# DeltaNet's q, k, v and z products: hi weights against both source halves in one 512-column matmul, in groups of four

## The chip, the cores and the metric

The kernel runs on one core of a Trainium2 chip. The metric is the device time of one execution in microseconds (us); several runs are taken and their median is compared. Five engines work side by side, each through its own instructions in order: TensorE (PE; its weight loads are listed as PEld), VectorE (DVE), ScalarE (ACT), GpSimd (POOL) and SyncE (SP), which issues most of the transfers.

## The reference, cut to what matters

A two-layer decoder trunk on 256 tokens of 2048 features. Layer 0 mixes tokens with an mLSTM, layer 1 with a gated DeltaNet; each layer then attends to 256 memory tokens and applies a squared-ReLU MLP. The change touches the DeltaNet:

```python
def gdn_mixer(h, w_in, conv_w, a_log, dt_bias, norm_g, w_out):
    p = h @ w_in                                   # 256 x 2048 times 2048 x 12352
    qkv, z, bt, a = jnp.split(p, GDN_SPLITS, axis=-1)
    qkv = jax.nn.silu(causal_dwconv(qkv, conv_w))  # 4 taps along the tokens
    q, k, v = jnp.split(qkv, [2048, 4096], axis=-1)
    q, k = l2_norm(q) * GD_K ** -0.5, l2_norm(k)   # 16 key heads of 128
    ...
    A = jnp.einsum('...id,...jd->...ij', kb, kc) * jnp.exp(jnp.where(strict, diff, -jnp.inf))
    U = lax.linalg.triangular_solve(A, vb, left_side=True, lower=True, unit_diagonal=True)
    ...
    o = rms_norm(from_chunks(oc), norm_g) * jax.nn.silu(z)
    return o.reshape(B, S, GV_H * GD_V) @ w_out
```

q and k have 2048 features each, v and z 4096 each.

## The kernel before, in words

**Numbers in two parts.** Weights and activations are float32, and a product is made of three: each operand is split into hi (rounded to the format that TensorE takes at full rate) and lo (what is left), and hi·hi + hi·lo + lo·hi is summed in a bank of PSUM. A source tile `srcs[k]` holds 128 features: hi of the 256 tokens in columns 0 to 255, lo in 256 to 511 (`T` is 256).

**Weights.** `Weights` streams them in units of 1 MB. For the DeltaNet's q (but its first four blocks), k, v and z a unit is "tall": all 2048 rows, 128 columns. It arrives in two halves of 1024 rows (SP's queue, four raw buffers); ACT casts each to hi (line 88), VectorE subtracts to get lo (line 89). Two units of hi and two of lo fit, so that a unit is split while the one before it is used.

**Products.** `prod_tall` takes one tall unit per block of 128 features: for each of 16 row blocks it loads hi or lo weights and multiplies, three times 256 columns, all into the first half of one bank of 512 columns. There are five such accumulators. `prod_feat`, which serves the other feature-major products (q, k, o of the mLSTM, up of the MLP), already works on the bank in two halves, "wide": hi weights times the whole source tile (512 columns), lo weights times hi of the source into the second half; `join` then sums the halves, with a copy by ACT and an addition by VectorE. For a block that is not wide, `join` returns the bank's first half and issues nothing.

**What follows a block.** For q, k and v: `conv` reads the joined block, times 1/rms, into `pad` (VectorE, line 865), makes four taps of the convolution (one by ACT, 868, three by VectorE, 870) and a silu by ACT (871). For z: a product by VectorE (1189) and a silu by ACT (1190).

**Stages of the DeltaNet.** For four groups c of key heads, four blocks of q, then four of k. Between them `norms` (l2 norms, by squares on ACT, 960, and matmuls, 964) and `pairs`, which makes the blocks of A for four value heads: `decays` (matmuls gep, exponentials by ACT, 939), the products of k and q (matmuls g, 981 and 982), masks and products on VectorE (984, 986, 992). The last of these run between the first v blocks. Then come 32 blocks of v, with the triangular solver's 31 steps on VectorE (1051, 1054) between the blocks' convolutions, and transposes of v to DRAM (884). Last, twice: 16 blocks of z in four groups, each with the `core` of four heads (a chain np, xp, wp, cp, op, otp of small matmuls with ACT and VectorE between them), and the output product `g_out`.

**Order.** Each engine's order is fixed when the program is built, by a scheduler that lists instructions by when it reckons them ready; independent matmuls are laid between the dependent ones of `pairs` and `core`. A waiting instruction holds up what stands behind it on its engine.

Of the kernel before, what the change touches and what calls it, by code (L numbers as in the profile page):

```python
# [15 lines left out]
T = 256  # L16
# [18 lines left out]
class Weights:  # L35
    """Streams weight units [128, kb, n] from DRAM and splits each into hi + lo."""
# [8 lines left out]
    def add(self, key, w, k0, kn, n0, nn, tall=False):  # L45
        """Units of 512 rows and 512 columns or, tall, of all the rows and 128 columns (64 at most: hi and lo side
        by side)."""
        kk, un = (kn, P) if tall else (UK * P, UN)
        for n in range(n0, n0 + nn, un):
            w_n = min(un, n0 + nn - n)  # L50
            for k in range(k0, k0 + kn, kk):
                self.plan.append((key, w[k : min(k + kk, k0 + kn), n : n + w_n]))

    def begin(self, place=None):
        """Starts the next unit's loads; returns the two halves' splits, to be called in order.
        place(j) gives other tiles to hold the unit: hi and lo of its j-th 128 rows."""
# [54 lines left out]
def trunk(ctx: ExitStack, tc, x, mem, norm_g, mem_norm_g, w_mem_kv, w_xq, w_xo, w_up, w_down,  # L111
# [56 lines left out]
    # rows j, columns i: j <= i, j < i, j > i  # L168
    tri_le, tri_lt, tri_gt = mask("tri_le", ALU.is_ge, 1), mask("tri_lt", ALU.is_gt, 1), mask("tri_gt", ALU.is_gt, -1)

    def behind(ins, *others):
        """Issue order on an engine: ins after each of the others."""
# [4 lines left out]
    # per-feature vectors as columns [128 features, 128-blocks]  # L177
# [27 lines left out]
    def feed(tok, c, h, gains, then=None):  # L205
        """Features 512 c .. of a token-major tile (t, 512 features): feature-major, gained and split into h."""
# [13 lines left out]
    class Rms:  # L220
        """Sums of squares along the features of token-major tiles [128 tokens, 512] by ACT."""
# [18 lines left out]
    def split_into(dst, src, scale=None):  # L240
        """dst[:, 0:256] = round(scale * src), dst[:, 256:512] = what is left."""
# [14 lines left out]
    def token_sums(parts, name):  # L256
        """Sums over the partitions of the parts' sum, as columns [128 tokens, 2]."""
# [11 lines left out]
    def spread(dst, col0, col1):  # L269
        """dst[p, t] = the token's scalar on every partition."""  # L270
        for t, c in enumerate((col0, col1)):
            PE.matmul(dst[:, t * P : (t + 1) * P], c.to_broadcast([P, P]), ident, start=True, stop=True)

    class Bank:
        """A block of a product: complete in the first 256 columns, or two parts in the two halves (wide)."""
# [4 lines left out]
    def extra_unit(u0):  # L280
        """Prepares one more unit of weights in tiles of u that are free around the end of a sub-layer."""
# [10 lines left out]
    def prod_feat(key, srcs, n_fb, evac, wide=True, before=None, fresh=False):  # L292
        """Feature-major product: srcs[k] = [128, hi 256 | lo 256]; evac(fb, bank).
        fresh: the sources are only being made, each one's hi first."""
# [30 lines left out]
    def prod_tall(key, srcs, n_fb, evac, before=None):  # L325
        """Feature-major product by tall units, one block after the other."""
        for f in range(n_fb):
# [4 lines left out]
            for k in range(nk):  # L332
                PE.matmul(a[:, 0:T], hi[k], srcs[k][:, 0:T], start=(k == 0), stop=False)  # L333
                PE.matmul(a[:, 0:T], hi[k], srcs[k][:, T:], start=False, stop=False)  # L334
                m = PE.matmul(a[:, 0:T], lo[k], srcs[k][:, 0:T], start=False, stop=(k == nk - 1))  # L335
            evac(f, Bank(a, False))
        return m

    def prod_few(key, srcs):
        """Product with n <= 64 columns, token-major: [128 tokens, 2, n] in PSUM."""  # L340
# [5 lines left out]
        # [I I] sums the rows of hi and lo  # L346
# [7 lines left out]
    def prod_tok(key, srcs, n_ch, evac, after=None, post=None, stagger=False):  # L354
        """Token-major product: evac(chunk, token tile, acc [128 tokens, 512]).
        stagger: in the last chunk the first token tile takes two units before the second one does."""
# [30 lines left out]
    def join(b, name, n=P, dst=None):  # L387
        """A product's block, summed over the halves of its bank."""
# [28 lines left out]
    class Scales:  # L417
        """1/rms per token: as columns (tok) and spread over the partitions (row)."""
# [13 lines left out]
    class Post:  # L432
        """Collects a sub-layer's output, token-major, with the gain of its norm, and its sums of squares."""
# [17 lines left out]
        def take(self, ch, t, a, plus=False):  # L451
            """A finished piece of the product (plus: what is there already)."""
# [39 lines left out]
    def advance(post, nxt):  # L492
        """x += g * y / rms(y); returns the next sub-layer's gained, not yet normalised input, and x's Rms."""
# [113 lines left out]
    def mlstm(sc, h, rms, before):  # L607
# [23 lines left out]
        # log sigmoid(f) = -log1p(e), e = exp(-f) >= exp(-15)  # L631
# [8 lines left out]
        # decayed scores, as [s, t] blocks: 0 = (s0, t0), 1 = (s1, t1), 2 = (s0, t1)  # L640
# [42 lines left out]
        def head_out(hd):  # L683
# [11 lines left out]
            # 1 / max(|den|, 1) and the head's 1/rms  # L695
# [39 lines left out]
    def cross(sc, l, h, rms):  # L735
# [44 lines left out]
        prod_tall("xq", h, 1, lambda f, a: ev_q(XA_H - 1, a))  # L780
# [4 lines left out]
    def mlp_bias(rms):  # L785
        """What the norm of the product's input adds to the mean square of its output's: eps + eps / (its rms^2)."""
# [43 lines left out]
    def softplus(z, sc, n):  # L830
        """log(1 + exp(z)), with log1p's accuracy for small exponentials."""
# [15 lines left out]
    def gdn(g0, h, rms):  # L847
        # Over all 256 tokens: (I + A) w = v, o = B w, with
# [399 lines left out]
```

## Time and profile before

| | us |
|---|---|
| median of three runs (lowest, highest) | 2963.81 (2963.45, 2971.68) |
| the profiled execution, first to last instruction | 2962.9 |
| DeltaNet: q, k and pairs | 1230 to 1543 |
| DeltaNet: v and solver | 1543 to 1690 |
| DeltaNet: z, core and output product | 1690 to 2100 |

The profile's span leaves out what lies before the first and after the last instruction; the median stands 0.9 us above it. In a row of the timeline stand the start in us, the time in us, engine, line, operation, the tiles (out<-in) and the shape; in square brackets the idle time of the engine before it, and what ended that. A matmul's time reaches from its start to its last result, and the next one starts before that: the rate is read from the distance of the starts. A row of groups has count, busy time in us and mean time of one in ns, then idle time before them.

### The profile page before, as it was taken

What the parts mean: (1) busy time and instruction counts of PE and PEld (TensorE: products, weight loads), DVE (VectorE), ACT (ScalarE), POOL (GpSimd) and SP (SyncE); (2) the same over time, 40 slices, a digit from 0 to 9 for tenths busy, and PEclk for the clock granted to TensorE, in tenths of its full rate; (3) what the DMA queues carried; (4) which work ended last, traced back from release to release, by engine and by line L of the source; (5) the groups of instructions that cost most, each with busy time, mean ns of one, the idle gap of its engine ahead of it and who ended that gap; (6) DMA issues with size and microseconds to landing.
All of it is one profiled execution on the core that took longest, in us unless ns stands there. A gap on an engine that the chain in (4) does not pass through costs nothing.

```text
span 2962.9 us, 43790 instructions
## 1 busy us (share of the span) xinstructions
PE 2912.0 (98%) x17363; PEld 2545.9 (86%) x17363; DVE 1762.6 (59%) x2560; ACT 1449.7 (49%) x2245; POOL 137.1 (5%) x256
## 2 busy tenths in 40 slices
PE   8999999999999999999999999999999999999998
PEld 7888888988888888898889998899888888888887
DVE  5555657644545555677779745445567546455565
ACT  6454546544434344566655444444456444344343
POOL 0000000000000000013231111000000000000000
PEclk9999999999999999999999999999999999999999
DMA  7545565555555565556778955665445565565554
GB/s 237 175 154 164 190 197 163 171 195 186 189 194 185 195 189 189 180 143 188 198 210 223 268 168 176 209 183 165 163 150 184 186 196 183 193 191 189 189 191 168
DMA packets 423120, 553.27 MB, mean 187 GB/s; under 512 B 22769, under 2 KB 220914, under 8 KB 420610
## 3 DMA queue, kind: packets, MB, share of 16 engines
q1 hardware_dynamic: 412608, 507.12, 55.5%
q0 software_dynamic: 8736, 42.02, 4.3%
q8 instruction: 136, 2.23, 0.3%
q10 hardware_dynamic: 1570, 1.33, 0.1%
q14 instruction: 70, 0.57, 0.1%
HBM read 527.29 MB, written 23.10 MB: 186 GB/s over the span
## 4 chain that ended last, share of the span: by engine, by line
PE 92%; DMA 3%; DVE 3%; ACT 2%; issue 1%; DVEq 0%; ACTq 0%; SPq 0%
PE up L314 15%; PE up L315 8%; PE down L378 8%; PE down L380 8%; PE down L379 8%; DMA raw<-in_gdn_w_in 3%; PE gz L334 2%; PE gz L335 2%; PE gz L333 2%; PE g_out L378 2%; PE g_out L379 2%; PE g_out L380 2%; PE o L314 2%; PE gv L333 1%; PE gv L334 1%; PE gv L335 1%
## 5 line engine op out<-in xcount | busy, mean ns | idle before, releaser
L89 DVE TENSOR_TENSOR lo<-raw,hi 128x1024 fp32r<-128x1024 f32 x938 | 1122.8, 1224 | 888.0 <-ACT hi L88 886.6
L88 ACT CAST hi<-raw 128x1024 fp32r<-128x1024 f32 x938 | 950.4, 1046 | 980.8 <-PE down L380 310.8
L314 PE MATMUL up<-h,hi 128*128 128x512 f32 x1920 | 678.7, 399 | 0.0
L315 PE MATMUL up<-h,lo 128*128 128x256 f32 x1920 | 539.2, 281 | 0.0
L314 PEld LDWEIGHTS up<-h,hi 128*128 128x128 f32 x1920 | 360.8, 188 | 89.9
L379 PE MATMUL down<-lo,u 128*128 128x512 f32 x1024 | 398.4, 389 | 0.0
L378 PE MATMUL down<-hi,u 128*128 128x512 f32 x1024 | 398.4, 389 | 0.0
L380 PE MATMUL down<-hi,u 128*128 128x512 f32 x1024 | 398.3, 389 | 0.0
L315 PEld LDWEIGHTS up<-h,lo 128*128 128x128 f32 x1920 | 362.7, 189 | 0.2
L380 PEld LDWEIGHTS down<-hi,u 128*128 128x128 f32 x1024 | 192.2, 188 | 40.0
L378 PEld LDWEIGHTS down<-hi,u 128*128 128x128 f32 x1024 | 192.2, 188 | 40.0
L379 PEld LDWEIGHTS down<-lo,u 128*128 128x128 f32 x1024 | 192.2, 188 | 39.7
L334 PE MATMUL gz<-h,hi 128*128 128x256 f32 x512 | 151.2, 295 | 0.0
L333 PE MATMUL gz<-h,hi 128*128 128x256 f32 x512 | 146.5, 286 | 2.5 <-ACT hi L88 2.5
L335 PE MATMUL gz<-h,lo 128*128 128x256 f32 x512 | 146.1, 285 | 0.8 <-DVE lo L89 0.8
L333 PE MATMUL gv<-h,hi 128*128 128x256 f32 x512 | 145.9, 285 | 0.5 <-ACT hi L88 0.5
L335 PE MATMUL gv<-h,lo 128*128 128x256 f32 x512 | 145.4, 284 | 0.0
L334 PE MATMUL gv<-h,hi 128*128 128x256 f32 x512 | 145.2, 284 | 0.0
L334 PEld LDWEIGHTS gz<-h,hi 128*128 128x128 f32 x512 | 97.8, 191 | 6.2 <-issue 6.2
L378 PE MATMUL g_out<-hi,u 128*128 128x512 f32 x256 | 100.9, 394 | 0.0
L379 PE MATMUL g_out<-lo,u 128*128 128x512 f32 x256 | 100.7, 393 | 0.0
L333 PEld LDWEIGHTS gz<-h,hi 128*128 128x128 f32 x512 | 97.9, 191 | 3.1 <-ACT hi L88 2.7
(415 smaller groups left out, 4889.0 us busy)
## 6 DMA issues: line engine op xcount, KB each, us to landing
raw<-in_w_up SPq DMA_DIRECT2D x256, 512.0 KB, 3.9
raw<-in_w_down SPq DMA_DIRECT2D x256, 512.0 KB, 4.0
raw<-in_gdn_w_in SPq DMA_DIRECT2D x192, 512.0 KB, 5.0
raw<-in_mlstm_w_in SPq DMA_DIRECT2D x96, 512.0 KB, 4.0
raw<-in_gdn_w_out SPq DMA_DIRECT2D x64, 512.0 KB, 4.4
raw<-in_mlstm_w_out SPq DMA_DIRECT2D x32, 512.0 KB, 4.5
at_d<-at POOLq DMA_DIRECT2D x8, 1536.0 KB, 7.6
ab<-at_d POOLq DMA_DIRECT2D x8, 1536.0 KB, 7.6
```

Source lines behind the costliest of these rows:

```text
L88: a = nc.scalar.copy(h_, raw[:, :, :n])
L89: return a, nc.vector.tensor_tensor(l_, raw[:, :, :n], h_, ALU.subtract)
L314: PE.matmul(a[:fw], wh, srcs[kk][:, :], start=(kk == 0), stop=False, skip_group_check=True)
L315: PE.matmul(a[:fw, T:], wl, srcs[kk][:, 0:T], start=False, stop=(kk == nk - 1), skip_group_check=True)
L333: PE.matmul(a[:, 0:T], hi[k], srcs[k][:, 0:T], start=(k == 0), stop=False)
L334: PE.matmul(a[:, 0:T], hi[k], srcs[k][:, T:], start=False, stop=False)
L335: m = PE.matmul(a[:, 0:T], lo[k], srcs[k][:, 0:T], start=False, stop=(k == nk - 1))
L378: PE.matmul(accs[t], sh, hi[j], start=(kk == 0), stop=False)
L379: PE.matmul(accs[t], sh, lo[j], start=False, stop=False)
L380: PE.matmul(accs[t], sl, hi[j], start=False, stop=(kk == nk - 1))
```

## The change

`prod_tall` becomes wide, in groups of four row blocks (`UK` is 4): four hi matmuls over 512 columns, then four lo matmuls over 256 columns into the bank's second half. The block is given on as wide, so that `join` issues its copy and its addition. The one other user of `prod_tall`, the last block of cross attention's q, keeps the old form.

```diff
-    def prod_tall(key, srcs, n_fb, evac, before=None):
+    def prod_tall(key, srcs, n_fb, evac, before=None, wide=True):
...
-            for k in range(nk):
-                PE.matmul(a[:, 0:T], hi[k], srcs[k][:, 0:T], start=(k == 0), stop=False)
-                PE.matmul(a[:, 0:T], hi[k], srcs[k][:, T:], start=False, stop=False)
-                m = PE.matmul(a[:, 0:T], lo[k], srcs[k][:, 0:T], start=False, stop=(k == nk - 1))
-            evac(f, Bank(a, False))
+            for k0 in range(0, nk, UK):
+                ks = range(k0, k0 + UK)
+                if wide:
+                    for k in ks:
+                        PE.matmul(a, hi[k], srcs[k][:, :], start=(k == 0), stop=False, skip_group_check=True)
+                    for k in ks:
+                        m = PE.matmul(a[:, T:], lo[k], srcs[k][:, 0:T], start=False, stop=(k == nk - 1),
+                                      skip_group_check=True)
+                    continue
+                for k in ks:
+                    PE.matmul(a[:, 0:T], hi[k], srcs[k][:, 0:T], start=(k == 0), stop=False)
+                    PE.matmul(a[:, 0:T], hi[k], srcs[k][:, T:], start=False, stop=False)
+                    m = PE.matmul(a[:, 0:T], lo[k], srcs[k][:, 0:T], start=False, stop=(k == nk - 1))
+            evac(f, Bank(a, wide))
...
-        prod_tall("xq", h, 1, lambda f, a: ev_q(XA_H - 1, a))
+        prod_tall("xq", h, 1, lambda f, a: ev_q(XA_H - 1, a), wide=False)
```

The function grows by ten lines, so that later lines of the program have numbers higher by ten after the change (its wide matmuls are lines 337 and 339, `join` is 407 and 409, `conv` 875 to 881).

The scheduler's order changes with it. Three places follow. First TensorE in a block of v (gv is the bank, h the source tiles by row block, hi and lo the unit's parts), before:

```order
L333 MATMUL gv_14205<-h_10289,hi_14109 128x256
L334 MATMUL gv_14205<-h_10289,hi_14109 128x256
L335 MATMUL gv_14205<-h_10289,lo_14110 128x256
L333 MATMUL gv_14205<-h_10290,hi_14109 128x256
L334 MATMUL gv_14205<-h_10290,hi_14109 128x256
L335 MATMUL gv_14205<-h_10290,lo_14110 128x256
```

The same place after:

```order
L337 MATMUL gv_14104<-h_10287,hi_14038 128x512
L337 MATMUL gv_14104<-h_10288,hi_14038 128x512
L337 MATMUL gv_14104<-h_10289,hi_14038 128x512
L337 MATMUL gv_14104<-h_10290,hi_14038 128x512
L339 MATMUL gv_14104<-h_10287,lo_14039 128x256
L339 MATMUL gv_14104<-h_10288,lo_14039 128x256
L339 MATMUL gv_14104<-h_10289,lo_14039 128x256
L339 MATMUL gv_14104<-h_10290,lo_14039 128x256
```

Three narrow matmuls per row block became one wide and one narrow, and lo is first needed after four wide ones.

Second, TensorE among the pairs of the third group of key heads (gep: decays; the bank gk_12192 belongs to one unit, gk_12260 to the next), before:

```order
L935 MATMUL gep<-gl_12389,tri_gt_r 128x512
L333 MATMUL gk_12192<-h_10283,hi_12114 128x256
L334 MATMUL gk_12192<-h_10283,hi_12114 128x256
L935 MATMUL gep<-gl_12391,tri_gt_r 128x512
L333 MATMUL gk_12260<-h_10275,hi_12182 128x256
L334 MATMUL gk_12260<-h_10275,hi_12182 128x256
L935 MATMUL gep<-gl_12400,tri_gt_r 128x512
L935 MATMUL gep<-gl_12402,tri_gt_r 128x512
L935 MATMUL gep<-gl_12400,ones_r 128x512
L935 MATMUL gep<-gl_12402,ones_r 128x512
L335 MATMUL gk_12192<-h_10283,lo_12115 128x256
```

The same place after:

```order
L945 MATMUL gep<-gl_12149,tri_gt_r 128x512
L337 MATMUL gk_11988<-h_10283,hi_11922 128x512
L337 MATMUL gk_11988<-h_10284,hi_11922 128x512
L337 MATMUL gk_11988<-h_10285,hi_11922 128x512
L337 MATMUL gk_11988<-h_10286,hi_11922 128x512
L945 MATMUL gep<-gl_12151,tri_gt_r 128x512
L337 MATMUL gk_12044<-h_10275,hi_11978 128x512
L337 MATMUL gk_12044<-h_10276,hi_11978 128x512
L337 MATMUL gk_12044<-h_10277,hi_11978 128x512
L337 MATMUL gk_12044<-h_10278,hi_11978 128x512
L945 MATMUL gep<-gl_12160,tri_gt_r 128x512
```

Where two narrow matmuls of a block stood between the decays' matmuls, four wide ones stand, and the lo matmul of the second unit moved further back.

Third, ACT at the start of the same pairs (l2sq: squares for the norms; gdm: the decays' exponentials; rk: the norms' roots), before:

```order
L960 ACTIVATE l2sq<-gqk_11038 128x512
L939 ACT_TABLE_LOAD
L939 ACTIVATE gdm<-gep,lnb 128x128
L871 ACT_TABLE_LOAD
L871 ACTIVATE gqk_11746<-cv 128x256
L266 ACT_TABLE_LOAD
L266 ACTIVATE rk<-l_12019,eps_t 128x8
L939 ACT_TABLE_LOAD
L939 ACTIVATE gdm<-gep,lnb 128x128 x7
L939 ACTIVATE gdm<-gep,sufb 128x128 x4
L988 ACTIVATE gm<-g_12082,rk 128x2x128
L88 CAST hi_12114<-raw_8_12118 128x1024
```

The same place after:

```order
L949 ACT_TABLE_LOAD
L949 ACTIVATE gdm<-gep,lnb 128x128
L878 ACTIVATE cv<-pad,cols 128x256
L266 ACT_TABLE_LOAD
L266 ACTIVATE rk<-l_11827,eps_t 128x8
L949 ACT_TABLE_LOAD
L949 ACTIVATE gdm<-gep,lnb 128x128
L881 ACT_TABLE_LOAD
L881 ACTIVATE gqk_11602<-cv 128x256
L949 ACT_TABLE_LOAD
L949 ACTIVATE gdm<-gep,lnb 128x128 x6
L949 ACTIVATE gdm<-gep,sufb 128x128 x4
```

The exponentials are cut once more, which costs a table load, and a convolution's step (878) moved ahead of them.

## The prediction

> **What bounds the kernel now.** I read the page first (the engines' busy shares and the chain that ended last), then the three stretches of the DeltaNet part in the view by stages, then single matmuls in order of time, and at the end the groups and waits of the engines around TensorE.
>
> ```profile
> span 2962.9 us, 43790 instructions
> ...
> PE 2912.0 (98%) x17363; PEld 2545.9 (86%) x17363; DVE 1762.6 (59%) x2560; ACT 1449.7 (49%) x2245; POOL 137.1 (5%) x256
> ...
> PE 92%; DMA 3%; DVE 3%; ACT 2%; issue 1%; DVEq 0%; ACTq 0%; SPq 0%
> ```
>
> TensorE is busy for 98% of the span and carries 92% of the chain, so a nanosecond saved per matmul is a nanosecond of time, wherever nothing else waits. The next view cuts the changed part into q and k with their pairs (up to 1543), the v blocks with the triangular solver (to 1690), and the z blocks with the heads' core and the output product (to 2100).
>
> ```profile
> core 0: us, PE busy (x) PEld busy (x) DVE busy (x) ACT busy (x) POOL busy (x), PEclk, DMA share, GB/s
> 1230.00:1543.30 313.30, 296.64 (x2229) 278.25 (x2228) 232.51 (x397) 200.05 (x360) 79.53 (x136) 0.98 0.65 177
> 1543.30:1690.00 146.70, 143.63 (x1199) 143.22 (x1199) 123.82 (x210) 71.36 (x106) 26.50 (x59) 1.00 0.84 243
> 1690.00:2100.00 410.00, 409.15 (x3212) 366.12 (x3213) 211.16 (x316) 194.11 (x286) 28.78 (x43) 1.00 0.59 178
> ```
>
> TensorE idles 16.7 us in the first stretch, 3.1 in the second, 0.9 in the third: outside the first, it sets the pace alone.
>
> **Step 1, the matmuls.** 92 blocks (12 of q, 16 of k, 32 of v, 32 of z) of 16 row blocks each are 1472 steps. Each step had three 256-column matmuls and gets one of 512 and one of 256: the same 768 columns with one instruction less. What an instruction costs beside its columns is read from starts in an undisturbed row of them. First and last of 60 narrow ones (gv), of 28 wide ones (down), of 12 pairs wide and narrow in turn (o), of 18 such pairs in another product (up):
>
> ```profile
> 1559.81 0.28 PE L333 MATMUL gv<-h,hi 128*128 128x256 f32 x1
> ...
> 1566.89 0.28 PE L335 MATMUL gv<-h,lo 128*128 128x256 f32 x1
> ```
> ```profile
> 999.69 0.39 PE L379 MATMUL down<-lo,u 128*128 128x512 f32 x1
> ...
> 1005.81 0.39 PE L379 MATMUL down<-lo,u 128*128 128x512 f32 x1
> ```
> ```profile
> 279.62 0.39 PE L314 MATMUL o<-h,hi 128*128 128x512 f32 x1
> ...
> 283.78 0.39 PE L314 MATMUL o<-h,hi 128*128 128x512 f32 x1
> ```
> ```profile
> 699.61 0.40 PE L314 MATMUL up<-h,hi 128*128 128x512 f32 x1
> ...
> 705.97 0.40 PE L314 MATMUL up<-h,hi 128*128 128x512 f32 x1
> ```
>
> Narrow: 7.08 us / 59 = 120.0 ns. Wide: 6.12 / 27 = 226.7 ns. So a column costs (226.7 - 120.0) / 256 = 0.417 ns, and each matmul 120.0 - 106.7 = 13 ns besides. Three narrow ones take 360 ns; a wide and a narrow one at these rates 346.7, and the pairs of o take 4.16 / 12 = 346.7 too. The pairs of up take 6.36 / 18 = 353.3, for no reason that I can see. The changed loop switches widths once in four steps where up switches at every step, so I charge a quarter of up's extra 6.6 ns: 348.4, a saving of 11.6 ns per step. 1472 x 11.6 ns = **-17.1 us**; the ends are 6.7 ns (up: -9.9) and 13.3 ns (o: -19.6). Per block it is 0.19 us.
>
> The Trainium skill (TensorE: Matmul & The Clock Gate, section Back-to-back issue gap) states a gap of N / 2.4 + 2.5 ns for isolated matmuls. By it a dropped matmul saves 2.5 ns, 1472 of them 3.7 us; the rows above, with 13 ns, disagree.
>
> **Step 2, the halves' sum.** A block was read straight from its bank by line 865 or 1189. Now ACT copies one half (join, line 397 of before), VectorE adds the other (399), and the old operation reads the sum.
>
> ```profile
> L397 ACT COPY h_up<-up x120: 357/370/374, 561.5 to 2867.8; 128x256 f32<-128x256 f32 x120
> L399 DVE TENSOR_TENSOR j_up<-up,h_up x120: 415/418/425, 563.0 to 2869.0; 128x256 f32<-128x256 f32 x120
> L865 DVE TENSOR_TENSOR pad<-gv,rb x32: 415/418/426, 1489.2 to 1693.8; 128x256 f32<-128x256 f32 x32
> L617 DVE TENSOR_TENSOR qk<-j_k,rb x8: 416/422/426, 130.9 to 158.3; 128x256 f32<-128x256 f32 x8
> ```
>
> The last two rows say that the old operation costs the same from a bank (418) and from a summed tile (422). New work: 92 x 0.370 = 34 us on ACT and 92 x 0.418 = 38.5 us on VectorE, 0.79 us in series behind each block. That tail delays no matmul by itself: a block takes 48 x 0.120 = 5.76 us, and there are five accumulators. What can delay matmuls is the next weights' split, since lo (line 89) queues on VectorE behind these adds and hi (line 88) on ACT behind these copies. That is charged where the queues are full.
>
> **Step 3, v and the solver.** Four periods of four v blocks:
>
> ```profile
> 1567.20:1591.10 23.90, 23.90 (x202) 23.90 (x201) 21.49 (x37) 12.48 (x20) 2.51 (x9) 1.00 0.86 244
> 1591.10:1615.00 23.90, 23.90 (x202) 23.90 (x201) 23.83 (x42) 11.95 (x18) 1.41 (x6) 1.00 0.73 196
> 1615.00:1638.90 23.90, 23.90 (x202) 23.90 (x201) 23.86 (x40) 12.36 (x20) 1.54 (x7) 1.00 0.68 191
> 1638.90:1662.80 23.90, 23.90 (x203) 23.90 (x201) 22.88 (x44) 12.64 (x19) 1.81 (x7) 1.00 0.77 211
> ```
>
> In the last three VectorE is already full: 1.1 us free out of 71.7. Twelve adds bring 5.0 us and TensorE runs 12 x 0.19 = 2.2 us faster, so the queue falls 5.0 + 2.2 - 1.1 = 6.1 us behind. Against it stands what lo is ahead of its use. At the tightest place I found, lo is done at 1627.73 + 1.22 = 1628.95 and used at 1630.34, 1.4 us later:
>
> ```profile
> 1627.73 1.22 DVE L89 TENSOR_TENSOR lo<-raw,hi 128x1024 fp32r<-128x1024 f32 x1
> ...
> 1630.34 0.28 PE L335 MATMUL gv<-h,lo 128*128 128x256 f32 x1
> ```
>
> In the new order the first lo matmul stands behind four wide ones (4 x 227 = 0.9 us) instead of two narrow ones (0.24), which gives 0.7 us more; and solver steps can slip into the first and next periods, which have room. Between 0 and 6.1 - 1.4 - 0.7 = 4.0 us; I take **+2**.
>
> **Step 4, q and k with their pairs.** Here TensorE does wait. The first group, and three matmuls of one such place (it comes four times, the last with v):
>
> ```profile
> L335 PE MATMUL gk<-h,lo 128*128 128x256 f32 x256 | 75.0, 293 | 5.2 <-DVE lo L89 5.2
> ...
> L333 PE MATMUL gk<-h,hi 128*128 128x256 f32 x256 | 74.4, 291 | 1.6 <-ACT hi L88 1.6
> ```
> ```profile
> 1331.28 0.38 PE L333 MATMUL gk<-h,hi 128*128 128x256 f32 x1 [0.53 <-ACT hi L88]
> ...
> 1333.90 0.39 PE L335 MATMUL gk<-h,lo 128*128 128x256 f32 x1 [0.56 <-DVE lo L89]
> ...
> 1338.86 0.38 PE L335 MATMUL gk<-h,lo 128*128 128x256 f32 x1 [1.20 <-DVE lo L89]
> ```
>
> VectorE is late there with lo, behind the pairs' products. Grouping lets TensorE pass: by the new order the work that stands ahead of the matmul that waited 1.20 us grows by about a dozen narrow matmuls' worth (four wide ones, of hi alone, where two narrow ones stood, at two places): up to 1.2 us, the whole of that wait, but not more than what is there. Four places: between 0 and -4.8, I take -3.5. Against it: the blocks between the start of the pairs and the wait, two at each place, end no earlier for being faster (8 x 0.19 = +1.5). And ACT gets a further table load at each place, ahead of the exponentials:
>
> ```profile
> 1322.00 1.28 ACT L939 ACT_TABLE_LOAD   x1
> ...
> 1328.48 0.47 ACT L988 ACTIVATE gm<-g,rk 128x256 f32<-128x256 f32 x1 [1.73 <-DVE gm L984]
> ...
> L868 ACT ACTIVATE cv<-pad,cols 128x256 f32<-128x256 f32 x64 | 32.2, 506 | 6.2 <-DVE pad L865 6.2
> ```
>
> ACT waits 1.73 us for VectorE after them, which covers the load (1.28) and nearly all of a convolution's step (0.51) that moved ahead too. If that cover is gone, hi comes late: at most 4 x 1.28 = 5.1 us. I take +0.5. Together **-1.5**, between +6.6 and -4.8.
>
> **Step 5, z and the core.** The core's steps wait for each other across engines, with z matmuls laid between:
>
> ```profile
> L1121 DVE SCALAR_TENSOR_TENSOR vt<-cp,nrk,vt 64x256 f32<-64x256 f32 x32 | 14.3, 489 | 45.5 <-PE cp L1136 45.5
> 1761.32 0.39 PE L334 MATMUL gz<-h,hi 128*128 128x256 f32 x1
> ...
> 1762.22 0.65 PE L1142 MATMUL wp<-vt,ti 64*64 64x128 f32 x4
> ```
> ```profile
> 1754.69 1.36 PE np L1100 x32
> ...
> 1792.62 1.36 PE np L1100 x32
> ```
>
> The core begins with np, so four z blocks and one core take 1792.62 - 1754.69 = 37.9 us. Six z matmuls need 0.72 us and the core's next step starts 0.90 us after the first of them, so part of this is latency of the core that no faster z shortens. About half of the z work lies inside the core; if half of that gains nothing, 8 cores x 64 steps x 11.6 ns x 1/4 = **+1.5** (between 0 and +3.0). ACT and VectorE are about half busy there (194 and 211 of 410 us) and hide their additions. Where z begins, matmuls wait for the split, and grouping gives back most of a lo wait of 0.8: **-0.7** (between 0 and -0.8).
>
> ```profile
> L335 PE MATMUL gz<-h,lo 128*128 128x256 f32 x512 | 146.1, 285 | 0.8 <-DVE lo L89 0.8
> ```
>
> Nothing else moves that TensorE waits for: the weights' loads are the same 990 instructions on SP, and of POOL's the v stores move a little.
>
> **The sum** against the profiled execution: 2962.9 - 17.1 + 2 - 1.5 + 1.5 - 0.7 = 2947.1 us. The median of the runs, 2963.81, lies 0.9 above the span; so 2948, rounded up to **2949 us** since more of the unknowns cost than give (-0.5%).
>
> **The rivals.** A measurement of this kernel tells a change from none at about 0.3%, 8.9 us: 2955 is the border of faster, 2973 of slower.
>
> - *Full queues give it back.* In the sixteen blocks of the four pair places and the twelve of the full solver periods, VectorE sets the pace: each add is paid (28 x 0.418 = 11.7) and the gain of these blocks is lost (28 x 0.19 = 5.3): -17.1 + 17.0 gives 2964. For it speaks the full queue of 1591 to 1663, against it VectorE's 80.8 us free before 1543.
> - *Slower.* VectorE is the pace in all 60 blocks of q, k and v: 60 x 0.418 = 25.1 us paid, and a gain left in z alone (32 x 0.19 = 6.1): 2964 + 19 = 2983. It decides from 62 paid adds on ((8.9 + 17.1) / 0.418). Against it: VectorE is busy for 356 of 460 us there, with the adds for 381 of some 449, 85%.
> - *The pitch does not fall.* Wide and narrow run as in up: -9.9 instead of -17.1, 2956. If a dropped matmul freed only a fifth of its 13 ns, the rest being bound to the columns, it is -3.8 for step 1 and 2962; only the rows of up point that way, and not so far. By the gap that the Trainium skill states (same page and section) the time would be this one too.
> - *More.* All waits of step 4 for hi and lo go (6.8 us instead of 3.5), with them two stretches at half clock. The clock falls in such places, in the window below by 0.06 x 29 = 1.7 us: 2949 - 3.3 - 3.4 = 2942.
>
> ```profile
> 1375.00:1404.00 29.00, 25.84 (x166) 22.18 (x165) 18.82 (x30) 22.55 (x44) 12.56 (x15) 0.94 0.37 106
> ```
>
> **How the numbers follow.** My forecast, with its own range 2943 to 2956: 0.52. Full queues: 0.20. Slower: 0.07. Pitch as in up 0.08, a fifth of it 0.03. More: 0.10. Faster: nearly all of the first, all of the last and a little of up's pitch, 0.62. Slower 0.08, same 0.30. The range 2941 to 2962 leaves out the slower case, the upper half of the full queues and some of the last case, under 0.2.
>
> **What would show it.** Right: in an undisturbed v block, 16 steps in about 5.57 us instead of 5.76; wide starts 227 to 236 ns apart, narrow 117 to 120. Step 2: adds and copies at 0.42 and 0.37 us, with TensorE busy through 1591 to 1663. Step 3 is wrong if matmuls of gv wait for lo by more than 4 us in sum. Step 4: the gk waits for lo fall from 5.2 to under 3; wrong if hi waits grow past 5 us or the exponentials start later. Step 5: the z period shortens from 37.9 us by 0.4 to 0.8. The forecast falls if wide matmuls take 240 ns here, or if VectorE's queue holds up TensorE through whole periods.

## The result, and the profile after

| | before | after |
|---|---|---|
| median of four runs (lowest, highest), us | 2964.82 (2963.45, 2971.68) | 2987.57 (2986.90, 2988.59) |
| the profiled execution, us | 2962.9 | 2985.2 |
| mean granted TensorE clock | 0.996 | 0.991 |

The change costs 0.72% (ratio 1.0072, 95% interval 1.0060 to 1.0085), 22.8 us by the medians and 22.3 between the profiled executions, where a gain of 15 was forecast. The page of after, span, engines and chain:

```profile
span 2985.2 us, 41114 instructions
...
PE 2916.3 (98%) x15891; PEld 2467.5 (83%) x15891; DVE 1790.2 (60%) x2652; ACT 1486.3 (50%) x2341; POOL 140.8 (5%) x256
...
PE 85%; DVE 6%; DMA 5%; ACT 2%; issue 2%; DVEq 0%; ACTq 0%; SPq 0%
```

TensorE's share of the chain fell from 92 to 85%; VectorE and transfers took it. The stages, cut at the first transposes of v, at the last gv, and at the point of g_out that corresponds to 2100 (before's first two cuts lie 1.6 and 3.6 us behind these events):

```profile
core 0: us, PE busy (x) PEld busy (x) DVE busy (x) ACT busy (x) POOL busy (x), PEclk, DMA share, GB/s
1230.00:1555.20 325.20, 299.25 (x1653) 248.95 (x1653) 242.72 (x428) 214.99 (x397) 83.16 (x136) 0.97 0.62 169
1555.20:1703.10 147.90, 142.57 (x808) 121.90 (x809) 131.96 (x233) 78.33 (x127) 21.48 (x52) 0.99 0.75 219
1703.10:2121.40 418.30, 411.41 (x2709) 338.63 (x2709) 219.07 (x349) 207.61 (x318) 33.92 (x50) 0.98 0.59 181
```

TensorE idles 26.0, 5.3 and 6.9 us in them (16.7, 3.1 and 0.9 before), and the clock, 0.98, 1.00 and 1.00 before, is lower in all three. The matmuls themselves did what was forecast. In an undisturbed v block (x4: four in a row):

```profile
1570.10 1.09 PE L337 MATMUL gv<-h,hi 128*128 128x512 f32 x4
1571.03 0.64 PE L339 MATMUL gv<-h,lo 128*128 128x256 f32 x4
1571.50 0.86 PE L337 MATMUL gv<-h,hi 128*128 128x512 f32 x3
```

Wide starts are 232 ns apart (0.93 / 4), narrow ones 118, a step takes 1.40 / 4 = 350 ns, which is also the median of the undisturbed steps of this trace: 10 ns saved of the 11.6 forecast, 14.7 us over 1472 steps. What grew is waiting. The waits of TensorE from 1230 on (columns: us in total, times, longest), three rows of after and the row of l before; the first row has no counterpart before:

```profile
PE g L992 <- DVE gm L996: 10.6, 4, 2.9
...
PE l L974 <- ACT l2sq L970: 6.9, 4, 1.9
...
PE gk L339 <- DVE lo L89: 5.1, 6, 1.1
```
```profile
PE l L964 <- ACT l2sq L960: 2.3, 3, 1.2
```

l L974, the sums of the norms, waits for ACT's squares, which stand behind the silu of a convolution that VectorE finishes late (the first time ACT idles 1.26 us for it). g L992 is the pairs' second product, `p1` in the code. Its bank is one of the three shared ones, and the matmul waits until the readers of an earlier g have let go of it. The last of the four at one place, with what VectorE and ACT do ahead:

```profile
1347.78 1.05 ACT L88 CAST hi<-raw 128x1024 fp32r<-128x1024 f32 x1 [1.93 <-DMA raw<-in_gdn_w_in]
1348.86 1.23 DVE L89 TENSOR_TENSOR lo<-raw,hi 128x1024 fp32r<-128x1024 f32 x1 [1.83 <-ACT hi L88]
...
1350.85 1.23 DVE L89 TENSOR_TENSOR lo<-raw,hi 128x1024 fp32r<-128x1024 f32 x1 [0.76 <-ACT hi L88]
...
1352.39 0.34 DVE L996 SCALAR_TENSOR_TENSOR gm<-g,rk,tri_lt 128x128 f32<-128x128 f32 x1
...
1354.63 0.34 DVE L996 SCALAR_TENSOR_TENSOR gm<-g,rk,tri_le 128x128 f32<-128x128 f32 x1
...
1355.12 0.67 PE L992 MATMUL g<-gqk 128*128 128x256 f32 x2 [2.60 <-DVE gm L996]
```

A masked product of 0.34 us stands on VectorE behind two weight splits; each split waits for ACT's hi, and hi waits for its transfer. VectorE idles 1.83 + 0.76 = 2.59 us at these splits (seven more short operations stand between the second split and the product), and TensorE stands still for 2.60 us, for transfers that it does not need yet.

In the first core a short operation of VectorE is late in the same way: tn, which xp reads, stands behind a split that waited 1.48 us for hi. The view puts xp's wait down to ACT's copy of v out of its bank, but that copy ended at 1737.45, and xp starts 0.10 us after the end of tn (1737.72 + 0.41 = 1738.13). Behind the wait the clock halves for 13.7 us:

```profile
1736.24 1.23 DVE L89 TENSOR_TENSOR lo<-raw,hi 128x1024 fp32r<-128x1024 f32 x1 [1.48 <-ACT hi L88]
...
1736.38 1.07 ACT L896 COPY v<-vp 128x512 f32<-128x512 f32 x2
...
1737.72 0.41 DVE L1112 TENSOR_TENSOR tn<-np,nrk 128x256 f32<-128x256 f32 x1
...
1738.23 0.87 PE L1121 MATMUL xp<-ti,tn 32*32 32x32 f32 x32 [2.67 <-ACT v L896]
```
```profile
1739.34:1753.00 13.66, 13.66 (x48) 9.87 (x47) 1.21 (x3) 1.69 (x4) 1.51 (x2) 0.50 0.36 106
```

That core takes 46.2 us to the next (37.9 before). The later ones take, by the chain of waits, 1816.47 - 1779.07 = 37.4:

```profile
1779.07 1.36 PE np L1110 x32
1816.47 1.36 PE np L1110 x32
```

### The profile page after: what moved, and what is told of

It is laid out like the page before. It is cut to its first block, busy times and chain, and to the rows that moved or that the text cites. A ratio compares the mean times of both kernels' runs of the same rounds, so it can differ in the third digit from the quotient of the medians.

```text
span 2985.2 us, 41114 instructions
## 1 busy us (share of the span) xinstructions
PE 2916.3 (98%) x15891; PEld 2467.5 (83%) x15891; DVE 1790.2 (60%) x2652; ACT 1486.3 (50%) x2341; POOL 140.8 (5%) x256
## 4 chain that ended last, share of the span: by engine, by line
PE 85%; DVE 6%; DMA 5%; ACT 2%; issue 2%; DVEq 0%; ACTq 0%; SPq 0%
PE up L314 15%; PE up L315 8%; PE down L388 8%; PE down L390 8%; PE down L389 8%; DMA raw<-in_gdn_w_in 5%; PE gz L337 4%; PE g_out L388 2%; DVE lo L89 2%; PE g_out L390 2%; PE gz L339 2%; PE g_out L389 2%; PE o L314 2%; PE wp L1152 1%; DVE cv L880 1%
## 5 line engine op out<-in xcount | busy, mean ns | idle before, releaser
L337 PE MATMUL gz<-h,hi 128*128 128x512 f32 x512 | 151.4, 407 | 3.5 <-ACT hi L88 3.5
L337 PE MATMUL gv<-h,hi 128*128 128x512 f32 x512 | 143.1, 401 | 0.3 <-ACT hi L88 0.3
L880 DVE SCALAR_TENSOR_TENSOR cv<-pad,cols,cv 128x256 f32<-128x256 f32 x192 | 93.9, 492 | 15.4 <-ACT cv L878 14.3
L337 PEld LDWEIGHTS gv<-h,hi 128*128 128x128 f32 x512 | 88.9, 191 | 15.3 <-ACT hi L88 2.2
L337 PEld LDWEIGHTS gz<-h,hi 128*128 128x128 f32 x512 | 87.0, 191 | 17.5 <-ACT hi L88 3.9
L388 PE MATMUL g_out<-hi,u 128*128 128x512 f32 x256 | 101.1, 395 | 0.0
L390 PE MATMUL g_out<-hi,u 128*128 128x512 f32 x256 | 100.4, 393 | 0.0
L339 PEld LDWEIGHTS gz<-h,lo 128*128 128x128 f32 x512 | 80.6, 191 | 15.1 <-issue 3.1
L339 PE MATMUL gz<-h,lo 128*128 128x256 f32 x512 | 91.0, 290 | 0.7 <-DVE lo L89 0.6
```

The source lines that it names most:

```text
L337: PE.matmul(a, hi[k], srcs[k][:, :], start=(k == 0), stop=False, skip_group_check=True)
L339: m = PE.matmul(a[:, T:], lo[k], srcs[k][:, 0:T], start=False, stop=(k == nk - 1), skip_group_check=True)
L388: PE.matmul(accs[t], sh, hi[j], start=(kk == 0), stop=False)
L390: PE.matmul(accs[t], sl, hi[j], start=False, stop=(kk == nk - 1))
L880: V.scalar_tensor_tensor(c, pad[:, j : j + T], w[j], c, ALU.mult, ALU.add)
```

## The experiments

My theory from here on: the scheduler's new order puts small operations that TensorE needs behind weight splits that wait for transfers; the stalls cost their length, and a stretch at half clock behind each long one. The rivals: the wide form itself, and the halves' sums on VectorE.

**One part at a time.** e1 leaves the second half of each q, k, v and z bank out of the result.

```diff
-            evac(f, Bank(a, wide))
+            evac(f, Bank(a, False))
```

> Wide and grouped matmuls, but the block is handed on as if it were complete in the bank's first half: no copy, no addition (this leaves the lo weights' part and the sources' lo part out of q, k, v and z). Theory 'the added copy and addition cost it, directly and through the order': the matmuls alone save the 17 us forecast, 2965 - 17 = 2948 (2943 to 2953). Rival 'the wide, grouped matmuls themselves cost it' (other order on TensorE, later lo): no gain without the additions either, 2970 or more.

Measured 2981.66, ratio 1.0053 (1.0038 to 1.0069). Without any of the 92 sums 16 of the 23 us are still lost: the sums as a load do not explain it alone.

e2 keeps the three narrow matmuls in their old order, puts two of them into the bank's second half, and sums.

```diff
-                        PE.matmul(a, hi[k], srcs[k][:, :], ...)
-                    for k in ks:
+                        PE.matmul(a[:, 0:T], hi[k], srcs[k][:, 0:T], ...)
+                        PE.matmul(a[:, T:], hi[k], srcs[k][:, T:], ...)
                         m = PE.matmul(a[:, T:], lo[k], srcs[k][:, 0:T], ...)
```

> Three narrow matmuls per step in the old order, but two of them go to the bank's second half and the block is copied and added as in the change. Theory 'copy and addition cost it': all of the loss and none of the gain, 2988 + 17 = 3005 (2995 to 3012). Rival 'the wide, grouped matmuls cost it': as before, 2965 (2960 to 2972).

2983.47, 1.0060 (1.0045 to 1.0075), between the two expectations. Either half of the change alone costs 16 to 18 us, both together 23: the parts do not add up. Both set off waits of g, which before has none: 12.5 us in e1, 5.7 in e2 (whose longest wait is another, gz for hi, 6.1).

e3, e4 and e12 make the change for z only, v only, q and k only (`wide=False` in the other calls of `prod_tall`).

> The change for z's 32 blocks alone. In the trace of the change three of four core periods of z got 0.5 us shorter, and the first one 8 us longer, after transposes of v and at half clock. Theory 'the first core's loss comes from v's stretch': z alone gains, 32 x 0.19 less a little, 2960 (2957 to 2963). Rival 'it is z's own': 2968 or more.

2962.61, 0.9990 (0.9981 to 1.0000): as the theory had it, though the gain of 2.7 us is at the edge of the noise.

> The change for v's 32 blocks alone. By the two traces v's stretch lost 12.7 us and the first core 8. Theory 'VectorE, full with the solver, cannot take the additions, and v's transposes and the first core pay for it': 2965 + 15 to 21 = 2980 to 2986. Rival 'the loss comes in from q and k, whose late VectorE work is passed on': 2962 to 2968.

2972.33, 1.0024 (1.0014 to 1.0033): between the two expectations.

> The change for q and k only. If the parts add up, the whole (+22) less v alone (+7) and z alone (-3) leaves +18: 2983. Theory (three of the four pair places have the g wait of 3 us with a half-clock window each behind it; the fourth has another order): 2978 to 2986. Rival (the loss comes from the parts together, through the fourth place and v's transposes): 2965 to 2973.

2974.56, 1.0030 (1.0019 to 1.0040), between the two; its trace has 7.8 us of g waits. z gains 3 us, v loses 7 and q with k 9, the whole loses more than the sum.

**Order alone.** e8 has before's three narrow matmuls and no sum, in groups of four: only the order changes.

```diff
                 for k in ks:
                     PE.matmul(a[:, 0:T], hi[k], srcs[k][:, 0:T], ...)
                     PE.matmul(a[:, 0:T], hi[k], srcs[k][:, T:], ...)
+                for k in ks:
                     m = PE.matmul(a[:, 0:T], lo[k], srcs[k][:, 0:T], ...)
```

> Three narrow matmuls as before, no halves' sum, but in groups of four row blocks (eight hi, then four lo). Only the order differs from before. Theory (order, not form): g stands after 88 units as in the slow kernels, waits for gm of 7 to 14 us, 2975 to 2992. Rival (the wide form or the sum costs the time): 2962 to 2968.

2975.79, 1.0033 (1.0018 to 1.0047): an order without wide matmul or sum costs 10 us. The same place in the timeline of before and of e8:

```profile
1343.65 0.34 DVE L984 SCALAR_TENSOR_TENSOR gm<-g,rk,tri_lt 128x128 f32<-128x128 f32 x1
...
1344.30 0.34 DVE L984 SCALAR_TENSOR_TENSOR gm<-g,rk,tri_le 128x128 f32<-128x128 f32 x1
...
1347.25 1.05 ACT L88 CAST hi<-raw 128x1024 fp32r<-128x1024 f32 x1 [5.12 <-DMA raw<-in_gdn_w_in]
...
1348.33 1.22 DVE L89 TENSOR_TENSOR lo<-raw,hi 128x1024 fp32r<-128x1024 f32 x1 [2.96 <-ACT hi L88]
...
1350.19 0.47 ACT L988 ACTIVATE gm<-g,rk 128x256 f32<-128x256 f32 x1
...
1351.52 0.59 PE L982 MATMUL g<-gqk 128*128 128x256 f32 x2
```
```profile
1346.10 1.05 ACT L88 CAST hi<-raw 128x1024 fp32r<-128x1024 f32 x1 [5.14 <-DMA raw<-in_gdn_w_in]
1347.18 1.23 DVE L89 TENSOR_TENSOR lo<-raw,hi 128x1024 fp32r<-128x1024 f32 x1 [3.24 <-ACT hi L88]
...
1350.15 1.22 DVE L89 TENSOR_TENSOR lo<-raw,hi 128x1024 fp32r<-128x1024 f32 x1
1351.68 0.34 DVE L994 SCALAR_TENSOR_TENSOR gm<-g,rk,tri_le 128x128 f32<-128x128 f32 x1
1352.06 0.47 ACT L998 ACTIVATE gm<-g,rk 128x256 f32<-128x256 f32 x1 [1.45 <-DVE gm L994]
...
1352.59 1.22 PE L992 MATMUL g<-gqk 128*128 128x256 f32 x2 [3.03 <-ACT gm L998]
```

In both, ACT waits 5.1 us for a transfer and VectorE about 3 for ACT. Before, both masked products lie ahead of that wait, and no g waits. In e8 one of them lies behind it, and TensorE waits 3.03 us. In these rows the difference is one instruction of 0.34 us that stands in another place of its queue.

e7 keeps wide and narrow in turn, without groups, with the sum.

```diff
                     for k in ks:
                         PE.matmul(a, hi[k], srcs[k][:, :], ...)
-                    for k in ks:
                         m = PE.matmul(a[:, T:], lo[k], srcs[k][:, 0:T], ...)
```

> The change without the groups of four: wide and narrow matmul in turn for each row block, with the halves' sum. In the order that comes out TensorE's g matmuls stand as before (after 22 and 94 units of gk, and three together), while the transposes of v are cut up more than after. Theory (place of the g matmuls and of their readers): g waits under 3 us, 2965 to 2978. Rival (the halves' sum or the wide form costs the time whatever the order): 2983 to 2992.

2992.37, 1.0087 (1.0071 to 1.0103). The expectation failed: TensorE's own order at g was that of before, yet g waited 6.5 us and l 9.7. So the place of the matmul on TensorE does not decide; the place of the readers on VectorE and ACT is what is left.

**Freeing the bank.** e5 and e6 take p1's bank from the accumulators; e6 also leaves the sum out, as e1 does.

```diff
-                    p0, p1 = psum("g0"), psum("g1")
+                    p0, p1 = psum("g0"), acc("g1")
```

> Wide, grouped matmuls without the halves' sum (the second half of each bank is left out of the result), and p1 in an accumulator bank. Theory: against the same without the bank (2981.7) the 13.9 us of g waits go and with them most of the 61 us at half clock: 2950 to 2960. Rival (the wide grouped form itself is slow here, by the clock): 2972 or more.

2965.41, 1.0000 (0.9990 to 1.0010): 16.3 us less than e1 by the bank alone, with 34.1 us at half clock instead of 61.4 (from 1230 to 2150). The waits of e1, then of e6:

```profile
PE g L992 <- ACT gm L998: 12.5, 4, 3.8
```
```profile
PE gq L337 <- ACT hi L88: 7.6, 4, 2.0
PE gz L337 <- ACT hi L88: 4.7, 1, 4.7
```

The g wait is gone; a wait of gq for hi came instead, and so the expected 2950 to 2960 was missed: the 14.7 us of the matmuls still do not show.

> The changed kernel, but the pairs' second product (p1) takes one of the five accumulator banks instead of one of the three shared ones, so that no g has to wait for the bank of an earlier g. Theory (the new order puts the reads of a g bank on VectorE and ACT behind weight splits that wait for their transfer, and TensorE waits 4 x 3 us at the next g, with half-clock windows behind it): the waits of g for gm fall from 11.2 us to under 2, half-clock time from 37.5 us to 15 to 25, time 2968 to 2975. Rival (VectorE and ACT have too much to do with the halves' sums, and TensorE only waits elsewhere): 2983 or more.

2994.04, 1.0091 (1.0076 to 1.0106): the rival was right. The g wait went, but with the sums on VectorE the time is waited elsewhere, and half clock rose from 37.5 to 58.0 us instead of falling:

```profile
PE gq L339 <- DVE lo L89: 6.6, 2, 3.5
PE gv L339 <- DVE lo L89: 5.9, 6, 3.1
PE vp L894 <- ACT gm L998: 5.0, 1, 5.0
```

**Taking load off VectorE.** e9 is the change for z and for the v blocks from the third group on (`wide=c > 1`), so that the order of q, k and the pairs is before's.

> The change for z and for the v blocks from the third group on (24 of 32), which lie beside the solver; q, k and the first two groups of v as before, so that TensorE's order in the pairs' stretch is that of before. Theory (two causes: the pairs' new order, and VectorE full beside the solver): the pairs' stretch is as long as before, and the late v blocks lose what the sums cost on VectorE: gv waits for lo of 3 to 8 us, v's transposes waiting for their convolution, 2962 to 2970. Rival (only the pairs' order costs anything): 24 x 0.19 = 4.6 us less than z alone (2962.6), about 2958.

2971.60 (2960.88 to 2974.14), 1.0014 (1.0002 to 1.0025). That is above both expectations, nearer to the theory, although gv waits only 1.8 us for lo. The pairs' stretch is as before (306.5 us); the profiled execution loses 9.3 us in the first core, where xp again waits 2.2 us, until VectorE's tn is done, and 17.1 us at half clock follow. It is the slowest of eleven executions; three of them, at a mean clock of 0.995 to 0.997 instead of its 0.992, took 2961 to 2965 us.

e10 and e11 let GpSimd multiply by 1/rms in the wide blocks, e10 in e9, e11 in the whole change with e5's bank.

```diff
-            padded.append(V.tensor_tensor(pad[:, 3:], d, rs.row, ALU.mult))
+            G.tensor_tensor(pad[:, 3:], d, rs.row, ALU.mult)
```

> The same, but for those v blocks GpSimd multiplies by 1/rms (line 875), so that VectorE does one operation per block as before (the sum) instead of two. Theory: VectorE has the room of before, the waits of gv for lo are under 2 us, 2955 to 2960. Rival (the form or the longer chain behind a block costs the time): no better than without it, 2962 or more.

2975.64, 1.0037 (1.0024 to 1.0049).

> The whole change with both reliefs: GpSimd multiplies by 1/rms in q, k and v (VectorE as busy as before), and p1 in an accumulator bank. Theory (the bank and VectorE's queue together hold the loss): as without the sums (2965), 2958 to 2970. Rival (the new order as a whole, whatever the bank and VectorE's load): 2980 or more, with waits in other places.

3010.54, 1.0146 (1.0130 to 1.0161). The theory failed in both. In e10 VectorE was relieved (from 1600 to 1685 it is busy for 72.0 us, 80.3 in e9), and yet gv waited 9.6 us for lo instead of 1.8. The row tells why: GpSimd takes 1.65 us (median) for what VectorE does in 0.42. ACT's step of the convolution waits for that, VectorE's steps wait for ACT (1.2 us at a time), and the splits stand behind them:

```profile
L879 POOL TENSOR_TENSOR pad<-j_cv,rb x24: 734/1646/2924, 1557.8 to 1711.6; 128x256 f32<-128x256 f32 x24
```

A queue with room can be late, too, when a short operation in it waits. How much VectorE's load counts by itself was not settled by these two.

e13 gives the last group's two v banks to the accumulators, in after. It goes by the view's word that xp waits for the copy of v.

```diff
-                vp = psum("vp")
+                vp = acc("vp") if c == 7 else psum("vp")
```

> The changed kernel, but the two banks of the last group's v transposes come from the accumulators, so that the first core's xp has no bank to wait for. TensorE's order is that of after. Theory: the 2.7 us of xp waiting for the copy of v and the 13.7 us at half clock behind it go, 2987.6 - 2.7 - 6.9 = 2978 (2975 to 2981). Rival (the first core is late for other reasons): 2985 or more, first core over 44 us.

2990.91, 1.0083 (1.0070 to 1.0097): the rival. xp waits 2.8 us for VectorE's tn, which stands behind lo, as it did in after, and the half clock stays (17.1 us); the first core takes 47.5 us. The bank was not what xp waited for.

**The price of a stall.** e15 and e16 are before with twelve stalls in the down products of the last MLP.

```diff
+                        d1 = PE.matmul(xb[:, 0:P], ident, ident, ...)
+                        S.copy(st[:, 0:P], xb[:, 0:P])
+                        # e15: two, e16: five more copies of st onto itself
+                        d2 = PE.matmul(xb[:, 0:P], st[:, 0:P], ident, ...)
+                        # the next matmul of either accumulator: behind d2
```

> The kernel before, with twelve stalls of TensorE in layer 1's down products: a small matmul, three copies by ACT, and a small matmul that the next products stand behind; about 1.5 us each. Theory (a 3.4 us stretch in which TensorE idles under about 1.8 us does not lower the clock): half-clock time as before within 7 us, added time 1.0 to 1.2 times the sum of the stalls, about +18 us. Rival (half clock follows any stall in proportion): added time 1.5 times the sum or more, +27.

2988.69, 1.0075 (1.0060 to 1.0090), 21.8 us more than before.

> The same with six copies by ACT in each chain, about 2.6 us a stall. Theory: at most places a stretch of 3.4 us at half clock follows (20 to 45 us more of it than before), and the added time is 1.3 to 1.8 times the sum of the stalls, +40 to +55 us. Rival (the half-clock stretches of the changed kernel have another cause than stalls): half-clock time as before, added time the sum of the stalls, +31.

3008.12, 1.0139 (1.0125 to 1.0153), 41.2 us more, within the theory's range. In the traces the stalls are shorter than I had reckoned, 1.02 and 2.00 us each (first row e15, second e16):

```profile
PE st L390 <- ACT st L389: 12.2, 12, 1.0
```
```profile
PE st L390 <- ACT st L389: 24.0, 12, 2.0
```

From the last matmul of g_out to the end of the program before takes 791.5 us, e15 812.5, e16 834.7. The twelve short stalls cost 21.0 and set off no half clock. That is 1.7 times their 12.2 us of idle time, not the 1.0 to 1.2 expected: the other 8.8 us go with the 24 small matmuls. The long ones cost 22.2 more: 11.8 of stall, and six stretches of 3.41 us at half clock, 10.2. One of the six, then a stall of the same 2.00 us that went free:

```profile
2425.40:2428.81 3.41, 1.41 (x9) 1.08 (x8) 0.78 (x1) 1.76 (x6) 0.00 (x0) 1.00 0.77 234
2428.81:2432.23 3.42, 3.42 (x10) 2.65 (x9) 0.00 (x0) 0.00 (x0) 0.00 (x0) 0.50 0.20 76
...
2374.20:2377.62 3.42, 2.39 (x12) 1.84 (x10) 2.36 (x2) 2.38 (x6) 0.00 (x0) 1.00 0.43 144
2377.62:2381.03 3.41, 2.44 (x12) 2.05 (x13) 0.00 (x0) 0.85 (x3) 0.00 (x0) 1.00 0.80 273
2381.03:2384.44 3.41, 3.41 (x17) 2.83 (x16) 1.47 (x2) 2.01 (x2) 0.00 (x0) 1.00 0.03 10
```

The clock's record changes on a grid of 3.413 us. A stall that lies in one cell (2.00 idle) halves the clock in the next; one that a cell border cuts (1.03 and 0.97) does not. So it went for all twelve: six within a cell with half clock, six cut, the larger part up to 1.64 us, without. In after it is the same with the four g waits: a border at 1353.63 cuts the first into 1.1 and 1.5 us, and no half clock follows; it follows the other three, with 2.2 to 2.7 us in one cell.

**What is worth keeping.** e14 is the change for z and for the third and the last group of v (`wide=c in (2, 7)`), beside which the solver has no steps.

> The change for z and for the eight v blocks of the third and the last group, beside which the solver has no steps; all else as before. Theory: 8 x 0.19 = 1.5 us less than z alone (2962.6): 2961, between 2958 and 2964. Rival (a change of the form in v costs a wait anywhere): 2966 or more.

2958.86, 0.9975 (0.9964 to 0.9985), within the theory's range: faster than both kernels, by 8 us against before. That it beats z alone is not shown: z alone gained 2.7 us against its own before, but the profiled executions of the two span 2956.6 us (e14) and 2956.0 (e3). The page of e14:

```profile
span 2956.6 us, 42618 instructions
...
PE 2905.9 (98%) x16723; PEld 2505.7 (85%) x16723; DVE 1773.7 (60%) x2600; ACT 1465.5 (50%) x2285; POOL 137.0 (5%) x256
```

## Where the time went, summed

For each profiled execution: the wide blocks' gain (0.16 us each, measured above), the change of TensorE's stalls from 1230 to the end of z (distance of starts beyond the usual pitch at that clock, from 0.1 us on, in front of matmuls for which the trace names a releaser; 24.5 us before), half the change of the time at half clock there (13.7 us before), their sum, and the measured span less 2962.9.

| | matmuls | stalls | half clock / 2 | sum | measured |
|---|---|---|---|---|---|
| after | -14.7 | +23.1 | +11.9 | +20.3 | +22.3 |
| e1 no sum | -14.7 | +14.0 | +23.9 | +23.2 | +18.4 |
| e2 sum only | 0 | +11.4 | +8.5 | +19.9 | +17.6 |
| e3 z | -5.1 | -1.8 | -1.7 | -8.6 | -6.9 |
| e4 v | -5.1 | +5.9 | +3.4 | +4.2 | +4.2 |
| e5 bank | -14.7 | +18.5 | +22.2 | +26.0 | +26.9 |
| e6 no sum, bank | -14.7 | +6.8 | +10.2 | +2.3 | +0.9 |
| e7 in turn | -14.7 | +21.8 | +15.4 | +22.5 | +24.4 |
| e8 order only | 0 | +5.3 | +8.5 | +13.8 | +12.2 |
| e9 late v, z | -9.0 | +7.0 | +10.2 | +8.2 | +9.5 |
| e10 e9, GpSimd | -9.0 | +11.8 | +3.4 | +6.2 | +9.7 |
| e11 bank, GpSimd | -14.7 | +32.7 | +23.9 | +41.9 | +46.5 |
| e12 q and k | -4.5 | +6.3 | +6.8 | +8.6 | +10.0 |
| e13 last v | -14.7 | +21.8 | +15.4 | +22.5 | +26.0 |
| e14 best | -6.4 | +1.1 | -1.7 | -7.0 | -6.3 |

The three terms give the time to within 5 us, mostly within 2.5. In after a third of what was lost is half clock.

## Why the prediction was wrong, step by step

- **Step 1** held: 350 ns a step instead of 348.4. Both rivals of the pitch are out (353.3 ns, and a fifth of the 13 ns), and so is the 2.5 ns per dropped matmul by the Trainium skill (TensorE: Matmul & The Clock Gate, section Back-to-back issue gap): it was 10.
- **Step 2** held in its prices, 0.358 for the copy and 0.418 for the addition:

```profile
L407 ACT COPY h_cv<-gk x16: 349/358/377, 1265.7 to 1486.7; 128x256 f32<-128x256 f32 x16
L409 DVE TENSOR_TENSOR j_cv<-gk,h_cv x16: 408/418/425, 1267.4 to 1487.1; 128x256 f32<-128x256 f32 x16
```

- **Step 3** (+2, at most +4) was too small: the stretch from the first transposes of v to the last gv grew by 3.1 us (144.7 to 147.8) although its 24 blocks are 3.8 faster, so it lost 6.9 (from event to event; the 12.7 in the expectation of e4 was another count). By the distance of starts gv waits 4.1 us for lo there, at the limit set (none before). For the rest there was no term: v's transposes wait 2.2 for the convolution (1.1 before, for the copy of v), and one cell at half clock costs 1.7.
- **Step 4** is the step that failed: -1.5, between -4.8 and +6.6 (the lower end leaves out the step's own +1.5). From the first gq to the first transposes of v the time grew by 15.7 us (306.5 to 322.2) although 36 faster blocks lie in it, 5.8 us of gain; so 21.5 were lost. The step costed the lo waits of gk, which did not move (5.2 before, 5.1 after, where under 3 was the sign of being right), and a table load. It had no term for g's bank: g waits 11.2 us by the distance of starts where 0 was. It had none for the norms, either: l waits for ACT's squares 4.8 us more (7.6 after, 2.8 before). The other stalls there are 2.3 us shorter, and 11.0 us more at half clock cost 5.5; together that is 19.2 of the 21.5. And the step took PE's new order as a gain, without asking where the order of VectorE and ACT had put the readers.
- **Step 5** held for the six later core periods, 0.5 us each, as said. It had no term for the first core, which gave 8.3 us back. Where z begins the wait for lo fell only from 0.8 to 0.6 us, and that for hi grew from 2.5 to 3.5.
- **The clock** stood in one rival only, as a gain. No step charged a stall with more than its length; in after that is 11.9 us.
- **The rivals.** The slower one (VectorE the pace in all 60 blocks, 2983) came near the time by luck, not by its mechanism: e1 has none of these additions and still takes 2982. The full queues that gave the gain back (2964) are a part of it at most: e9, with the sums beside the solver, loses 6 us, and e8, with no sums, 10.

Left open: how much of the loss with the sums is VectorE's queue by itself (e10 and e11 do not tell; freeing g's bank helped without the sums, in e6, and not with them, in e5), and what wide q and k would bring in before's order of VectorE and ACT, which no kernel here kept.

## What to carry to other kernels

Where a scheduler sets the order, look after a change of a hot loop not at that loop but at the short operations around it: on every in-order engine, which reader of a scarce bank now stands behind an instruction that waits for a transfer. Price a stall of TensorE by its length and, where about 2 us or more of it fall into one cell of 3.4 us, by a stretch at half clock behind it, about 1.7 us more; in this kernel that is an estimate from twelve stalls of 2.00 us. When a view names who ended a wait, see whether that one had ended just then. A change that is good where the helper engines have room (z: 0.5 us a period) can be kept for these places alone.

## What the runs showed of the hardware

- Over sixteen traces of this kernel (1230 to 2150 us), cells of the 3.413 us grid in which TensorE idled 2.2 us or more at full clock were followed by half clock in 39 of 39 cases, 1.8 to 2.2 us in 22 of 28, 0.3 to 1.8 us in 30 of 302, less in 7 of 3768. Of the 37 with less than 1.8 us, 31 hold the norms' l matmuls of two columns each, which count as busy: idle time alone does not set the clock, and what else does stays open. At half clock, all 26 cells with 0.6 us or more idle were followed by another, 33 of 132 with less, which is how one stall of 2.7 us became 13.7 us at half clock in the first core. The Trainium skill (TensorE: Matmul & The Clock Gate, section What's actually happening) states that the window runs freely and that the clock falls after at least one idle window of about 3.4 us. The grid agrees; that a window must be idle as a whole does not, 2.00 us within one were enough.
- At half clock (after, from 1423.15 on) four wide matmuls take 1.71 us from start to start, 427 ns each, which is twice the 213 ns of their columns (512 x 0.417) and not twice the 232: the fixed part does not show there.
- GpSimd's product of 128x256 took from 0.73 to 2.92 us beside a busy VectorE (e10), against VectorE's 0.42 us for the same.
